# The last local head's four blocks tied behind the first four product steps, and the preceding head's blocks up to two a strip

## The chip, the cores and the metric

The kernel runs on one core of one Trainium2 chip. The metric is device time in microseconds of one launch; the time before is the median of three runs, 2186.0 us (2185.98 to 2188.91). Five engines of the core matter here: TensorE (PE for its matmuls, PEld for its weight loads), VectorE (DVE), ScalarE (ACT), GpSimd (POOL) and SyncE (SP), which issues all of this kernel's DMAs. Each engine runs its own instructions in the order in which they stand in its queue, and waits at an instruction until what it needs is there.

## The reference

One encoder layer is applied to a prompt of 1024 tokens and a sample of 256 tokens, each with 16 learned meta tokens in front. Eight heads attend globally (two key and value heads, rotary positions), eight heads attend to a neighbourhood of 8 x 16 grid cells and to the meta tokens. Both halves are gated and go through one output projection.

```python
def encoder_layer(h, norm_w, w_in, ..., rpb, w_out, rope_tabs):
    u = rms_norm(h, norm_w) @ w_in.astype(h.dtype)
    qa, ka, va, za, qb, kb, vb, zb = jnp.split(u, split_points(), axis=-1)
    ...
    ya = global_gqa(qa, ka, va) * jax.nn.silu(za)
    ...
    yb = neighbourhood_attention(qb, kb, vb, rpb) * jax.nn.silu(zb)
    y = jnp.concatenate([ya, yb], axis=-1) @ w_out.astype(h.dtype)
    return h + y
```

Here `qb`, `kb`, `vb`, `zb` are the query, key, value and gate of the eight local heads, 128 wide each.

## The kernel before

All products of the projections are made in three matmuls of a high and a low part each (`split`, L59: ACT casts the high part at L61, DVE subtracts for the low part at L62).

**Strips.** The input projection runs in two chunks of tokens. In each, a strip is one 128-wide slice of `w_in`, for instance the q of one head. `strips` (L176) loads and splits its weights in four pieces and multiplies them with all tokens of the chunk; in the second chunk a strip has two blocks of tokens (512 and 272 wide), so two PSUM tiles `pp`. An evacuation follows: `qk_evac` (L215) for q and k squares the strip on ACT (L218), sums over the partitions on POOL (L220), goes on with DVE and ACT (L221, L68 to L73), scales on DVE (L237) and stores the result in DRAM (L240); `z_evac` (L256) makes the gate.

**Chunk 2.** `chunk2` (L686) first does the global heads, and after each of these one strip of the list `late`. That list holds, for each local head, its strips v, k, q, z in this order (`VB`, `KB`, `QB_`, `ZB`); 24 of its 32 strips are left when the loop at L860 begins. I call the last four of them V7, K7, Q7 and Z7, after local head 7; they are strips 20 to 23 of that loop.

**Local blocks.** `local_blocks` (L820) is a generator over the eight local heads (0 to 7), four blocks each. A block is `attend_strip` (L416): four score products (L438) and the products with the meta tokens (L272, L273) into the PSUM tiles `sp` (two buffers); evacuation on DVE (L276, L443) into the tiles `S` (five buffers, two a block); the maximum by DVE and POOL (L452, L455, L282, L284); exponentials (L460, L463, L290); the sum (L452, L455, L299, L301); value products into `po` (L467, L470; one buffer); and `put_y` (L304), which ends with DVE's L318 and the store of y (L319). `load(h)` issues a head's loads: k from what K's strip stored (L777 to L780), v (L736), the bias table (L478), q (L789, L790) and z (L797); q is split anew on ACT and DVE after its load. The tiles of k, q and the table have one buffer each, so the loads for one head wait for the blocks of the head before. v's two tiles hold two blocks' windows each.

The loop at L860 projects one strip and then runs blocks as long as `done * n < 28 * (i + 1)`: 28 blocks over 24 strips. The 28th is head 6's last and is followed by `load(7)` inside the same step of the generator.

**Output projection.** `outproj` (L988) does the projection in seven products by a scheme that saves one of eight (`order = (1, 2, 5, 6, 7, 3, 4)`), each in ten steps; `step n` is 24 matmuls (`products`, L943: L949 to L951) into one PSUM tile `pq`. Two steps share one y tile (`y_load`, L880, `y_operand`, L894), and y tiles take turns in four buffers. Product 1 (steps 0 to 9) needs the global heads only; product 2 (from step 10) needs y of the local heads, where tile 0 (steps 10 and 11) holds blocks 0 and 1 of each head and tile 1 (steps 12 and 13) blocks 2 and 3. A step's weights `wm` are loaded into the tiles of the strips' input `xb` (L926) as these come free, and split. After steps 3 to 9 the generator is asked for a block, which is where head 7's four blocks are traced: behind steps 3, 4, 5 and 6.

**Order.** The program is written once in this traced order; a scheduler then orders each queue by a model of the time at which each instruction would be ready, with the traced order as priority, so that an instruction can be placed ahead of others that were traced before it. `issue_after(x)` adds one rule to it: instructions traced inside stand behind `x` in the queue of `x`'s engine. From step 10 on `in_order` (L869) keeps each queue in traced order.

Of the kernel before, what the change touches and what calls it, by code (L numbers as in the profile page):

```python
# [35 lines left out]
NH = 8  # L36
# [11 lines left out]
NT = TH // P  # L48
# [6 lines left out]
class Kern:  # L55
# [630 lines left out]
    def chunk2(self):  # L686
        nc, io = self.nc, self.io
# [16 lines left out]
        def k_strip(s, g, wc, rope):  # L704
            k, km = k_first(g)

            def evac(ps):
                for p, (o, n) in zip(ps, BL):
                    rp = (ct[:, o:o + n], st[:, o:o + n]) if rope else None
                    self.qk_evac(p, o, n, wc, rp, [(0, n, k[:, 0, C1P + o:C1P + o + n], k[:, 1, C1P + o:C1P + o + n])])  # L710
                return k, km
            return s, BL, evac

        def v_rows_of(s, g):

            def evac(ps):
                for p, (o, n) in zip(ps, BL):
                    self.rows_out(self.v_rows(p, o, n), n, self.vn[g], C1P + o)
            return s, BL, evac
# [9 lines left out]
        def v_windows(h):  # L729

            v = []
            for i in range(2):
                t = self.v.tile([P, 8, P], F32, tag=f"v{i}", name="vw", align_bytes=ALIGN)
                for j in range(2):
                    o = 32 * WIN0[2 * i + j]
                    nc.sync.dma_start(t[:, 4 * j:4 * j + 4, :], self.vn[2 + h][:].rearrange("(t p) d -> p t d", t=4)[o:o + P])  # L736
                    v.append(t[:, 4 * j:4 * j + 4, :])
            return v, self.load_vm(2 + h)
# [37 lines left out]
        def k_load(g):  # L776
            k = self.k.tile([P, NP + NMETA], F32, tag="k1", name="kfull", align_bytes=ALIGN)  # L777
            nc.sync.dma_start(k[:, :C1P], self.kfd[g][:, :C1P])
            nc.sync.dma_start(k[:, C1P:NP], self.k2d[g][:])
            nc.sync.dma_start(k[:, NP:], self.kfd[g][:, C1P:])  # L780
            km = self.k.tile([P, 8, NMETA], F32R, tag="km", name="km")[:, :7]
            full = [k[:, NP:].unsqueeze(1).to_broadcast([P, n, NMETA]) for n in (4, 3)]
            nc.scalar.copy(km[:, :4], full[0])
            nc.vector.tensor_tensor(out=km[:, 4:], in0=full[1], in1=km[:, :3].bitcast(F32), op=ALU.subtract)
            return k, km.rearrange("p c m -> p (c m)")

        def q_load(h):
            qf = self.qf.tile([P, NP], F32, tag="qf", name="qfull")
            nc.sync.dma_start(qf[:, :C1P], self.qfd[h][:])  # L789
            nc.sync.dma_start(qf[:, C1P:], self.q2d[h][:])  # L790
            q = self.q.tile([P, 2, NP], F32R, tag="q", name="q", align_bytes=ALIGN)
            self.split(q[:, 0, :], q[:, 1, :], qf[:])
            return q, qf

        def z_load(h):
            z = self.z.tile([P, NP], F32, tag="z", name="z")
            nc.sync.dma_start(z[:], self.zd[h][:])  # L797
            return z
# [4 lines left out]
        def run_block(h, b, q, z, k, v, tab):  # L803
            k, km = k
            v, vm = v
            if tab is not None:
                c = slice(64 * b, 64 * b + 64)
                q, qf = q
                self.attend_strip(q, qf, strips_of(z[:])[:, :, c], k, km, v[b], vm[:], tab, b,
                                  self.yd[1][:, b // 2:NP // P:2, h - 8, 64 * (b % 2):64 * (b % 2) + 64])  # L810
                return
            c = slice(QB * b, QB * b + QB)
            keys = [(k[:, 0, o:o + P], k[:, 1, o:o + P]) for o in range(0, NP, P)]
            self.attend(q[:, :, c], z[:, c], keys, km, v, vm[:], self.yd[0][:, 2 * b:2 * b + 2, h, :])
# [5 lines left out]
        def local_blocks():  # L820
            def load(h):
                k, v = k_load(2 + h), v_windows(h)
                tab, q, z = self.bias_table(h, "bt", (3, 384)), q_load(8 + h), z_load(8 + h)
                return q, z, k, v, tab

            tiles = load(0)
            for h in range(NH):
                for b in range(4):
                    run_block(8 + h, b, *tiles)
                    if b == 3 and h + 1 < NH:  # L830
                        tiles = load(h + 1)
                    yield

        pr = self.project
# [10 lines left out]
        for g in range(2):  # L845
            if g == 0:
                k, _ = pr(k_strip(KA, 0, kw, True), v_rows_of(VA, 0))
            else:
                k, = pr(k_strip(KA + g, g, kw, True))
                pr(v_rows_of(VA + g, g))  # L850
            v = v_tiles(g)
            for h in range(4 * g, 4 * g + 4):
# [3 lines left out]
                fill(FILL)  # L856

        self.blocks = local_blocks()
        n, done = len(late), 0
        for i in range(n):  # L860
            fill(1)
            while done < 4 * (NH - 1) and done * n < 4 * (NH - 1) * (i + 1):
                next(self.blocks)
                done += 1

# [75 lines left out]
    def products(self, ws, y):  # L943
        nc = self.nc
        ps = self.pq.tile([P, FB], F32, tag="pq", name="pq")
        for k in range(8):
            wh, wl = ws[k][:, 0, :], ws[k][:, 1, :]
            yh, yl = (a[k // WCH][:, k % WCH, :] for a in y)
            nc.tensor.matmul(ps[:], yh, wh, start=k == 0, stop=False)  # L949
            nc.tensor.matmul(ps[:], yh, wl, start=False, stop=False)  # L950
            nc.tensor.matmul(ps[:], yl, wh, start=False, stop=k == 7)  # L951
        return ps[:]

    def out_sums(self, p, i, ps, o):
# [33 lines left out]
    def outproj(self, end_attention):  # L988
        self.U, self.V = {}, {}
        order = (1, 2, 5, 6, 7, 3, 4)  # L990
        N = 2 * NT * len(order)

        def step(n):
            q, r = divmod(n, 2 * NT)
            return order[q], *divmod(r, 2)

        def tile_of(m):
            return order[m // NT], m % NT

        M = NT * len(order)  # L1000
        yr, ys, wr, ws, x, out = {}, {}, {}, {}, {}, {}

        def load_y(m):
            if m < M and m not in yr:
                yr[m] = self.y_load(*tile_of(m))

        def make_y(m):
            if m < M:
                load_y(m)
                ys[m] = self.y_operand(*tile_of(m), yr.pop(m))  # L1010

        def load_w(q, j):
            if q < len(order):
                wr[q, j] = self.w_load(order[q], j)

        def make_w(q, j):
            if q < len(order):
                ws[q, j] = self.w_operand(wr.pop((q, j)))

        load_y(0)  # L1020
        for j in range(16):
            if j == 12:
                load_y(1)
            load_w(0, j)
        make_y(0)
        for j in range(16):
            make_w(0, j)
        traced = None
        for n in range(N):
            p, t, b = step(n)  # L1030
            q, m = n // (2 * NT), n // 2
            if n == 2 * NT - 1:
                for _ in self.blocks:
                    pass
            if n == 2 * NT:
                end_attention()
                traced = len(self.nc.cur_bb.bb.instructions)
            if n - 2 in out:
                self.store(out.pop(n - 2), *step(n - 2))
            last = t == NT - 1  # L1040
            if NT - 3 <= t < NT - 1:
                with self.tc.issue_after(self.lasty):
                    for j in range(4):
                        load_w(q + 1, 8 * (t - NT + 3) + 4 * b + j)
            if q:
                for i in (n, n + 1, n + 2):
                    if i < N and i not in x:
                        x[i] = self.x_load(*step(i))
            direct = m + 1 < 2 * NT
            if direct:  # L1050
                (load_y, make_y)[b](m + 1)
            elif m + 2 < M:
                load_y(m + 2)
            if b == 0 and not direct:
                make_y(m + 1)
            ps = self.products([ws[q, 8 * b + k] for k in range(8)], ys[m])
            if last:
                for k in range(8):
                    make_w(q + 1, 8 * b + k)
            o = self.out_sums(p, 2 * t + b, ps, x.pop(n, None))  # L1060
            if o:
                out[n] = o
            if 2 < n < 2 * NT:
                next(self.blocks, None)
            if traced:
                traced = self.in_order(traced)
        for n in sorted(out):
            self.store(out[n], *step(n))
# [158 lines left out]
```

## Time and profile before

| what | value |
|---|---|
| median of three runs | 2186.0 us (2185.98 to 2188.91) |
| the profiled execution, whole | 2188.16 us |
| its span | 2186.4 us |
| granted TensorE clock, mean | 0.997 |
| TensorE busy | 2156.9 us, 99% of the span |
| DVE, ACT, POOL busy | 75%, 51%, 24% |
| matmuls of the strips 512 wide (L210 to L212) | 1664 a line, mean 0.39 us each |
| matmuls of the output projection (L949 to L951) | 560 a line, mean 0.39 us each |
| chain that ended last | TensorE 90%, DVE 3%, DMA 3% |

A timeline row holds the start and the length in us, the engine, the line, the operation, what it writes and reads, and how many instructions were merged; square brackets hold the engine's idle time just before and what released it. Matmuls overlap: one lasts 0.39 us though the next starts after 0.23. A window row holds, for a stretch of the span, its length and then the busy time (and the number of instructions) of PE, PEld, DVE, ACT and POOL, the granted clock as a share of full speed, the busy share of the DMA engines and GB/s. SPq rows are the issues of DMAs, which land some microseconds later. A group row holds line, engine, operation, tiles and count, then busy time in us and the mean of one in ns, then idle time before them.

### The profile page before, as it was taken

How to read it: one execution, taken by the hardware profiler on the slowest of the kernel's cores; microseconds unless marked ns; L12 is line 12 of the kernel's file. 1: busy time of each engine (PE TensorE's matmuls, PEld its weight loads, DVE VectorE, ACT ScalarE, POOL GpSimd, SP SyncE). 2: the span in 40 equal slices, each digit the busy share in tenths (PEclk: the TensorE clock that was granted, in tenths of full speed). 3: DMA queues.
4: the chain of work that ended last, by engine and by line, in shares of the span. 5: the costliest groups of instructions: out<-in, count | busy, mean ns of one | idle time of the engine just before them, and what ended most of it. 6: DMA issues, size and time to landing. Idle time of an engine off the chain costs nothing.

```text
span 2186.4 us, 34153 instructions
## 1 busy us (share of the span) xinstructions
PE 2156.9 (99%) x11736; PEld 1880.3 (86%) x11736; DVE 1644.7 (75%) x2991; ACT 1120.0 (51%) x2294; POOL 521.8 (24%) x249
## 2 busy tenths in 40 slices
PE   8999999999999999999999999999999989999999
PEld 7888888888888999998999999898889978788887
DVE  8687976787864889996799989777677686455763
ACT  6556544545554766665666666444444454232230
POOL 1232422222211233231233225333223221000000
PEclk9999999999999999999999999999999999999999
DMA  8767889988554333334233334654433463763663
GB/s 295 225 196 229 278 281 325 349 266 268 171 191 140 105 104 113 117 107 143 95 113 108 110 121 156 187 158 128 130 124 113 125 207 96 243 235 112 225 228 106
DMA packets 263614, 383.83 MB, mean 176 GB/s; under 512 B 45040, under 2 KB 113296, under 8 KB 263440
## 3 DMA queue, kind: packets, MB, share of 16 engines
q1 hardware_dynamic: 263440, 381.65, 53.9%
q8 instruction: 92, 1.51, 0.3%
q14 instruction: 82, 0.67, 0.1%
HBM read 281.01 MB, written 100.38 MB: 174 GB/s over the span
## 4 chain that ended last, share of the span: by engine, by line
PE 90%; DVE 3%; DMA 3%; ACT 1%; SPq 1%; issue 1%; POOL 1%; POOLq 0%; DVEq 0%; ACTq 0%
PE pp L210 20%; PE pp L212 20%; PE pp L211 20%; PE pq L949 6%; PE pq L951 6%; PE pq L950 6%; PE sp L438 2%; PE po L470 2%; PE sp L334 1%; PE sp L333 1%; PE sp L332 1%; PE po L372 1%; PE po L373 1%; PE po L374 1%; SPq L227 0%
## 5 line engine op out<-in xcount | busy, mean ns | idle before, releaser
L210 PE MATMUL pp<-x,wh 128*128 128x512 f32 (+1 forms) x1664 | 653.6, 394 | 6.3 <-ACT wh L61 6.2
L212 PE MATMUL pp<-x,wl 128*128 128x512 f32 (+1 forms) x1664 | 649.4, 391 | 0.2 <-DVE wl L62 0.2
L211 PE MATMUL pp<-x,wh 128*128 128x512 f32 (+1 forms) x1664 | 649.5, 391 | 0.0
L210 PEld LDWEIGHTS pp<-x,wh 128*128 128x128 f32 x1664 | 313.1, 188 | 63.0 <-ACT wh L61 7.5
L212 PEld LDWEIGHTS pp<-x,wl 128*128 128x128 f32 x1664 | 313.1, 188 | 62.1 <-DVE wl L62 1.2
L211 PEld LDWEIGHTS pp<-x,wh 128*128 128x128 f32 x1664 | 313.5, 188 | 52.1
L220 POOL PARTITION_ALL_REDUCE m<-ms x78 | 232.6, 2982 | 363.6 <-ACT ms L218 326.3
L62 DVE TENSOR_TENSOR wl<-wr,wh 128x512 fp32r<-128x512 f32 (+1 forms) x290 | 213.7, 740 | 131.0 <-ACT wh L61 104.2
L301 POOL PARTITION_ALL_REDUCE tot<-a x80 | 172.8, 2161 | 487.2 <-DVE a L299 466.9
L61 ACT CAST wh<-wr 128x512 fp32r<-128x512 f32 (+1 forms) x290 | 174.5, 607 | 199.2 <-PE pp L211 179.0
L211 PE MATMUL pp<-xb,wh 128*128 128x272 f32 x832 | 241.4, 290 | 0.0
L210 PE MATMUL pp<-xb,wh 128*128 128x272 f32 x832 | 240.0, 288 | 0.0
L212 PE MATMUL pp<-xb,wl 128*128 128x272 f32 x832 | 239.5, 288 | 0.0
L949 PE MATMUL pq<-wm,yh 128*128 128x512 f32 x560 | 219.7, 392 | 3.7 <-ACT yh L61 3.7
L951 PE MATMUL pq<-wm,yl 128*128 128x512 f32 x560 | 219.0, 391 | 0.0
L950 PE MATMUL pq<-wm,yh 128*128 128x512 f32 x560 | 218.8, 391 | 0.0
L284 POOL PARTITION_ALL_REDUCE ma<-m x80 | 107.6, 1345 | 440.8 <-DVE m L282 432.0
L210 PEld LDWEIGHTS pp<-xb,wh 128*128 128x128 f32 x832 | 156.6, 188 | 7.3
L211 PEld LDWEIGHTS pp<-xb,wh 128*128 128x128 f32 x832 | 156.5, 188 | 7.1
L212 PEld LDWEIGHTS pp<-xb,wl 128*128 128x128 f32 x832 | 157.4, 189 | 0.1
L949 PEld LDWEIGHTS pq<-wm,yh 128*128 128x128 f32 x560 | 105.8, 189 | 26.3 <-ACT yh L61 4.5
L951 PEld LDWEIGHTS pq<-wm,yl 128*128 128x128 f32 x560 | 105.5, 188 | 22.4 <-DVE yl L62 0.7
(207 smaller groups left out, 3845.0 us busy)
## 6 DMA issues: line engine op xcount, KB each, us to landing
wr<-in_w_in SPq DMA_DIRECT2D x414, 256.0 KB, 3.5
wld<-wl SPq DMA_DIRECT2D x132, 256.0 KB, 4.3
wl<-wld SPq DMA_DIRECT2D x132, 256.0 KB, 3.1
yr<-yd SPq DMA_DIRECT2D x35, 512.0 KB, 5.1
wq<-in_w_out SPq DMA_DIRECT2D x64, 256.0 KB, 5.2
td<-wq SPq DMA_DIRECT2D x64, 256.0 KB, 4.5
ww<-td SPq DMA_DIRECT2D x64, 256.0 KB, 5.3
ww<-in_w_out SPq DMA_DIRECT2D x48, 256.0 KB, 5.2
```

The lines of the kernel that those rows point to most:

```text
L61: self.hi = nc.scalar.copy(hi, full).ins
L62: return nc.vector.tensor_tensor(out=lo, in0=full, in1=hi.bitcast(F32), op=ALU.subtract).ins
L210: nc.tensor.matmul(p[:, :n], wh[:, k, :], xh[:, :n], start=first, stop=False)
L211: nc.tensor.matmul(p[:, :n], wh[:, k, :], xl[:, :n], start=False, stop=False)
L212: nc.tensor.matmul(p[:, :n], wl[:, k, :], xh[:, :n], start=False, stop=last)
L220: nc.gpsimd.partition_all_reduce(m2[:], ms[:], P, RED.add)
L284: nc.gpsimd.partition_all_reduce(ma[:], m1[:], P, RED.max)
L301: nc.gpsimd.partition_all_reduce(tot[:], a1[:], P, RED.add)
L438: nc.tensor.matmul(dst, k[:, o:o + P], qfv[:, a:e, :], start=True, stop=True)
L949: nc.tensor.matmul(ps[:], yh, wh, start=k == 0, stop=False)
L950: nc.tensor.matmul(ps[:], yh, wl, start=False, stop=False)
L951: nc.tensor.matmul(ps[:], yl, wh, start=False, stop=k == 7)
```

## The change

```diff
@@ local_blocks
                 for b in range(4):
                     run_block(8 + h, b, *tiles)
-                    if b == 3 and h + 1 < NH:
+                    if b == 3 and h + 2 < NH:
                         tiles = load(h + 1)
+                    yield
+                if h + 2 == NH:
+                    tiles = load(h + 1)
                     yield
@@ chunk2
             fill(1)
-            while done < 4 * (NH - 1) and done * n < 4 * (NH - 1) * (i + 1):
+            while done < 4 * (NH - 1) and done * n < 4 * (NH - 1) * (i + 1 + max(0, i + 5 - n) / 3):
                 next(self.blocks)
                 done += 1
+        next(self.blocks)
@@ products
-            nc.tensor.matmul(ps[:], yl, wh, start=False, stop=k == 7)
+            self.lastmm = nc.tensor.matmul(ps[:], yl, wh, start=False, stop=k == 7).ins
@@ outproj
-            if 2 < n < 2 * NT:
-                next(self.blocks, None)
+            if n < 2 * NT:
+                with self.tc.issue_after(self.lastmm):
+                    next(self.blocks, None)
```

Three things change. `load(7)` becomes a step of its own of the generator, taken after the last strip. The bound of the loop rises over the last four strips: with 24 strips, 25 blocks are done after strip 20 as before, then 27 instead of 26 after strip 21 (K7), 28 instead of 27 after strip 22 (Q7), and none is left for strip 23 (Z7). And head 7's four blocks are traced behind steps 0, 1, 2 and 3 of the output projection instead of 3, 4, 5 and 6, with their TensorE instructions kept behind the last matmul of that step in TensorE's queue; the other engines' instructions of a block are not tied. The instructions themselves, their number and their operands stay what they are.

## The prediction, made before the changed kernel ran

> **What bounds the kernel now.** I began with the page's first part.
>
> ```profile
> span 2186.4 us, 34153 instructions
> PE 2156.9 (99%) x11736; PEld 1880.3 (86%) x11736; DVE 1644.7 (75%) x2991; ACT 1120.0 (51%) x2294; POOL 521.8 (24%) x249
> ```
>
> TensorE is busy for all but 29.5 us of the span, and the change takes no matmul away. So it can win only idle time of TensorE and the half-clock time behind it. The view of waits, TensorE alone, says where the idle time is (total us, times, longest).
>
> ```profile
> PE sp L438 <- DVE m L452: 9.0, 1, 9.0
> PE pp L210 <- ACT wh L61: 6.2, 2, 5.4
> PE pq L949 <- ACT yh L61: 3.7, 1, 3.7
> PE tp L253 <- DVE vm L62: 1.7, 1, 1.7
> ```
>
> Two single waits, 9.0 and 3.7 us, lie on what the diff touches: a score matmul of a local block (L438) and a product step (L949). The view of windows gives the granted clock (behind the POOL column) after these two waits and after the one of 1.7 us.
>
> ```profile
> 1782.16:1786.12 3.96, 3.96 (x13) 3.65 (x14) 3.17 (x7) 2.39 (x5) 0.07 (x1) 0.50 0.29 98
> 1864.86:1868.01 3.15, 3.15 (x7) 2.43 (x8) 2.69 (x5) 0.62 (x1) 0.00 (x0) 0.50 0.81 283
> 612.65:618.00 5.35, 5.25 (x33) 4.66 (x34) 3.68 (x8) 1.95 (x4) 1.43 (x1) 1.00 0.53 165
> ```
>
> After the 9.0 us wait 3.96 us run at clock 0.50, which costs half of that, 1.98; after the 3.7 us wait 3.15 us, which costs 1.58; after 1.7 us of idleness nothing. With the waits' own 9.02 and 3.69 (rows below) the two places lose 16.3 us. That is the most the change can win at them.
>
> **The first wait.** The timeline of TensorE around it:
>
> ```profile
> 1752.09 0.61 PE L438 MATMUL sp<-qfull,kfull 128*128 128x128 f32 x4
> ...
> 1769.80 0.28 PE L467 MATMUL po<-Pm,vm 128*128 128x256 f32 x1
> ...
> 1771.64 0.61 PE L438 MATMUL sp<-qfull,kfull 128*128 128x128 f32 x4
> ...
> 1782.16 2.47 PE L438 MATMUL sp<-qfull,kfull 128*128 128x128 f32 x8 [9.02 <-DVE m L452]
> ...
> 1784.86 0.63 PE L949 MATMUL pq<-wm,yh 128*128 128x512 f32 x1
> ```
>
> I number the 32 local blocks in the order traced: 25 to 28 are head 6's, 29 to 32 head 7's. The rows at 1752.09 and 1771.64 are the scores of blocks 27 and 28, each behind a strip (Q7 and Z7, the last two); 1769.80 is block 27's value product. At 1782.16 stand block 29's scores, ahead of product step 0 (1784.86). TensorE runs its queue in order, so step 0 waits too. Was it ready? The vector engine's groups in the stretch of strip Z7, 1752.25 to 1771.64, say yes:
>
> ```profile
> L62 DVE TENSOR_TENSOR wm<-ww,wm 128x512 fp32r<-128x512 f32 x9 | 6.8, 771 | 0.0
> ...
> L62 DVE TENSOR_TENSOR yl<-yl,yh 128x512 fp32r<-128x512 f32 x2 | 1.3, 672 | 0.0
> ```
>
> Nine of the 16 weight splits and both halves of the first y tile start there; step 0 needs eight and those two. It sits out a wait that isn't its own.
>
> The releaser named, L452, doesn't feed L438. The timeline of the other engines and of the DMA queue shows whose wait it is:
>
> ```profile
> 1757.82 0.40 ACT L218 ACTIVATE ms<-pp 128x272 f32<-128x272 f32 x1
> ...
> 1776.65 0.49 DVE L237 SCALAR_TENSOR_TENSOR rs_r<-pp,nqkw,rs_r 128x272 f32<-128x272 f32 x1
> ...
> 1777.16 0.32 SPq L240 DMA_DIRECT2D q2d<-rs_r  x1
> ...
> 1778.90 0.32 SPq L790 DMA_DIRECT2D qfull<-q2d  x1
> ...
> 1782.10 1.04 ACT L61 CAST q<-qfull 128x1024 fp32r<-128x1024 f32 x1 [3.73 <-DMA qfull<-q2d]
> ```
>
> This is the second piece of head 7's q: squared out of PSUM at 1757.82, finished by DVE at 1777.14, stored, loaded again from 1778.90, landed when ACT's cast starts at 1782.10, 0.06 us ahead of the matmul. It is slow because DVE is full: the windows of strips Q7 and Z7 and of the gap (DVE is the third column of busy time).
>
> ```profile
> 1733.76:1752.25 18.49, 18.49 (x109) 16.51 (x108) 14.54 (x29) 8.30 (x19) 6.97 (x5) 1.00 0.28 87
> 1752.25:1771.64 19.39, 19.39 (x116) 17.38 (x115) 17.04 (x31) 12.93 (x26) 8.44 (x4) 1.00 0.68 235
> 1771.64:1782.16 10.52, 1.50 (x12) 1.23 (x11) 10.52 (x23) 6.71 (x16) 0.61 (x1) 0.70 0.69 241
> ```
>
> **The change, part by part.**
>
> *The tie.* Block 29's matmuls now follow step 0's last one in TensorE's queue. A step is 24 matmuls; a window of 100 us that holds nothing but product steps prices one at 100/440 = 0.227 us:
>
> ```profile
> 1900.00:2000.00 100.00, 100.00 (x440) 82.17 (x439) 53.13 (x76) 32.81 (x60) 0.00 (x0) 1.00 0.49 177
> ```
>
> So a step of 5.5 us moves into the gap. The wait does not vanish. Count from the scores behind strip Q7 (block 27's now, block 28's then, the same work): to the end of Z7 19.55 us (1752.09 to 1771.64), with step 0 25.0. The q tile lands 1782.10 - 1752.09 = 30.0 after the same point. I place block 29's scores right behind step 0, since the scheduler had them ready even ahead of it; they find 5.0 us still missing. Idle time falls from 9.02 to 5.0: gain 4.0. Step 0 has those 5 us of slack, so a late start of its own costs nothing up to there, and one for one beyond.
>
> Is the clock cold after 5.0 us? After 1.7 us it was not, after 3.69 it was; 5.0 lies beyond the second, so the 1.98 us stay. The Trainium skill, "TensorE: Matmul & The Clock Gate", Part 1: The HAM clock gate, has the array fall to half rate after an idle window of about 3.4 us; by it a rest just under that would stay warm, and the sum would then come out near 2173 us (an estimate from that page: 9.02 - 3.4 + 1.98 + 5.27 = 12.9 off 2186.0). The rows above agree with that window.
>
> *Two blocks behind strip K7, one behind Q7, none behind Z7.* Blocks 27 and 28 move up a strip; matmuls, vector and ACT work only change place. Block 28's scores go ahead of Z7 from behind it, which delays Q7's end and the q chain equally, so the count above holds. What it can cost is DVE time in strip Q7's stretch: a block's 17 vector instructions at some 0.42 us (L318's row, below) are 7.1 us, and that stretch has 18.49 - 14.54 = 3.95 free. At worst 3.2 us spill into the q chain, and the rest becomes 8.2; at best the chain has block 27's last rows out of its way and shortens by 2. I take zero: the loop's present rule already puts two blocks behind strips 0, 6, 12 and 18 (28(i + 1)/24, rounded up, rises by two there), and the list above has no entry for them. Around strip 18:
>
> ```profile
> L438 PE MATMUL sp<-qfull,kfull x32: 271/300/326, 1630.7 to 1677.1; 128*128 128x128 f32 x16, 128*128 128x192 f32 x16
> ```
>
> Four blocks of eight score matmuls in the 60 us from 1620, which hold some 3.2 strips.
>
> *load(7) as a step of its own behind the last strip.* It issues twelve DMAs: three for k, four for v, two for q, one each for vm, the bias table and z, all on SP's queue. What held k and q's first piece was block 28's scores; these would end some 18 us sooner, so k, that piece and the table (five issues, at L790's 0.32 us and up some 2 us) can pass ahead of the 16 w_out and four y loads. Bounds: nothing if SP is idle there, 2 us and the transfers' time if not, which step 0's slack covers. q's second piece still hangs on the store at 1777.16. I take zero.
>
> *Blocks 30 to 32 behind steps 1 to 3 instead of 4 to 6.* Today they already come one a step, at no wait:
>
> ```profile
> 1792.51 0.28 PE L467 MATMUL po<-Pm,vm 128*128 128x256 f32 x1
> ...
> 1815.17 0.61 PE L438 MATMUL sp<-qfull,kfull 128*128 128x128 f32 x4
> ...
> 1821.98 0.61 PE L438 MATMUL sp<-qfull,kfull 128*128 128x128 f32 x4
> ...
> 1829.24 0.60 PE L438 MATMUL sp<-qfull,kfull 128*128 128x128 f32 x4
> ...
> 1829.80 0.28 PE L467 MATMUL po<-Pm,vm 128*128 128x256 f32 x1
> ```
>
> 6.8 and 7.3 us apart: a step and a block each. I take zero.
>
> **The second wait** hangs on block 32's end:
>
> ```profile
> 1845.55 12.63 SPq L319 DMA_DIRECT2D yd<-y  x2
> ...
> 1857.37 0.42 DVE L318 SCALAR_TENSOR_TENSOR y<-y,r 128x256 f32<-128x256 f32 x1
> ...
> 1859.74 0.91 SPq L890 DMA_DIRECT2D yl<-yd  x2
> ...
> 1864.19 0.62 ACT L61 CAST yh<-yl 128x512 fp32r<-128x512 f32 x1 [8.05 <-DMA yl<-yd]
> ...
> 1864.86 0.79 PE L949 MATMUL pq<-wm,yh 128*128 128x512 f32 x1 [3.69 <-ACT yh L61]
> ```
>
> Block 32's y is done at 1857.79; its store and the one before hold SP's queue for 12.63 us; step 12's y tile is loaded only at 1859.74; its cast at 1864.19 releases L949. Three steps earlier is 16 us, less the 5 of rest; 4 would do. With no store ahead the load waits for its buffer alone, which step 9 frees two steps (11 us) before step 12. All of 3.69 + 1.58 = 5.27 goes. Next in line would be step 14's tile, which has the same 11 us.
>
> **Sum.** 4.0 + 5.27 = 9.3 us. The profiled execution took 2188.16 us, 1.76 of it around its span, and would take 2178.9. The median of the three runs, 2186.0, lies 2.2 lower; on that scale the forecast is **2176.7**.
>
> **Rivals.**
>
> A, *no wait left*: block 29's scores come behind step 1, or the q chain gains 5 us. For it: step 1's 5.5 us cover the 5.0. Against: the scheduler had those scores ready ahead of step 0, so they should follow it at once. Price: all 16.3 go, 2169.7.
>
> B, *the first gap stays*: the second block or the loads that pass push q or step 0's weights out by 4 us (the bounds above add to 5.2), and only the second wait goes: 2186.0 - 5.3 = 2180.7.
>
> C, *slower: the S buffers set the pace*. There are five, two a block, so block n+2 can't leave PSUM whole before block n's value product, and blocks advance one per half of the time from scores to value product. That time is 14.6 us for block 30 (1815.17 to 1829.80) but 20.9 for block 28 on a full DVE (1771.64 to 1792.51). At 20.9 the pace is 10.4 us against some 6.9 for a step with its block: 3.5 us of wait for each of blocks 30 to 32, and 1.6 of cold clock each time, 15.3 in all: 2186.0 - 9.3 + 15.3 = 2192.0. It decides from about 15 us on. For it: head 7 now starts while DVE still finishes Z7. Against: blocks 30 to 32 kept the pace without a wait. The Trainium skill, "TensorE: Matmul & The Clock Gate", Architectural detail, calls ACT's and DVE's queues strictly first in, first out, by which one waiting cast holds a block's whole chain; no row here contradicts it.
>
> D, *no change*: the scheduler pulls other work with a wait of its own into the gap, 2186.
>
> **Chances.** Forecast 0.52, A 0.20, B 0.14, C 0.08, D 0.06. A measurement of this kernel tells some 0.2%, 4.4 us, from no change: under 2181.6 is faster, over 2190.4 slower. The forecast, A and a third of B are faster: 0.77. C and a little of the tail of B and D are slower: 0.09. The rest, 0.14, is the same. The range runs from just under A, 2168.5, over the forecast's worst spill (3.2: 2179.9) and B to 2184; C, D and the tails of A and B lie outside. The forecast's own range is 2173 to 2180.
>
> **What would show it.** Right: step 0's first L949 directly behind strip Z7; then a rest of 3 to 7 us ahead of block 29's scores, still released by q's load, and clock 0.50 after it; no wait at step 12; TensorE idle for about 21.8 us of the span instead of 29.5. Wrong: block 29's scores behind step 1 (A), a wait for wm ahead of step 0 (B), waits at L438 or L467 between steps 1 and 6 (C).

## The result, and the profile after

| | before | after |
|---|---|---|
| median of six runs each | 2185.99 us | 2180.05 us |
| ratio, with its 95% interval | | 0.9966 [0.9956, 0.9975] |
| the profiled execution, its span | 2188.16, 2186.4 us | 2181.10, 2179.3 us |
| TensorE idle in the span | 29.5 us | 23.2 us |

The change is faster by 5.9 us of median, where 9.3 were forecast (2176.7); the profiled span is 7.1 us shorter. The lines of the products' matmuls are now L953 to L955, and a y tile's load is L894. The page's first part, of the kernel after:

```profile
span 2179.3 us, 34152 instructions
...
PE 2156.1 (99%) x11736; PEld 1881.0 (86%) x11736; DVE 1644.8 (75%) x2991; ACT 1120.7 (51%) x2294; POOL 520.8 (24%) x249
```

Of the 7.1 us, 6.3 are idle time of TensorE that is gone and 0.8 are busy time. Not all of it belongs to the change: strip Q7 starts behind the same 9742 matmuls in both kernels, at 1733.00 us after and at 1733.76 before, so 0.8 us had been gained before any moved block ran. The view of waits, TensorE alone, shows which (total us, times, longest):

```profile
PE po L467 <- DVE Pm L294: 6.8, 1, 6.8
PE pp L210 <- ACT wh L61: 5.4, 1, 5.4
...
PE sp L273 <- DVE q L62: 0.9, 1, 0.9
...
PE pq L953 <- ACT yh L61: 0.4, 1, 0.4
```

The second wait (3.69 us at step 12) is gone; the 0.4 us of the last row stand at a later step, at 1913.99 us. Of the first, 9.02 us at L438, 0.9 us are left at L273, but a new wait of 6.8 us stands at L467, a block's value product. TensorE's timeline around it:

```profile
1779.12 0.55 PE L467 MATMUL po<-Pm,vm 128*128 128x256 f32 x1 [6.79 <-DVE Pm L294]
...
1781.35 0.88 PE L953 MATMUL pq<-wm,yh 128*128 128x512 f32 x1
...
1787.42 0.60 PE L438 MATMUL sp<-qfull,kfull 128*128 128x128 f32 x4
...
1789.25 0.37 PE L273 MATMUL sp<-q,km 128*112 128x256 f32 x1 [0.89 <-DVE q L62]
```

Z7 ends at 1772.33. Behind it stands not step 0, as forecast, but the value product of block 28, head 6's last; step 0 (1781.35) follows it, and block 29's scores (1787.42) follow step 0. Why is block 28's Pm (its probabilities of the meta tokens) late? Rows of DVE, POOL and ACT from the timeline:

```profile
1765.45 0.40 DVE L282 TENSOR_TENSOR m<-m,Sm 16x256 f32<-16x256 f32 x1
...
1766.03 5.40 POOL L284 PARTITION_ALL_REDUCE ma<-m  x1 [3.40 <-DVE m L282]
...
1771.45 0.43 DVE L459 TENSOR_TENSOR S<-S,ma 128x256 f32<-128x256 f32 x1 [0.96 <-POOL ma L284]
...
1774.16 1.88 DVE L62 TENSOR_TENSOR wm<-ww,wm 128x512 fp32r<-128x512 f32 x3
...
1775.44 0.40 ACT L293 CAST Pm<-Sm 48x256 fp32r<-48x256 f32 x1
...
1778.56 0.41 DVE L294 TENSOR_TENSOR Pm<-Sm,Pm 16x256 fp32r<-16x256 f32 x1
...
1781.02 0.49 DVE L237 SCALAR_TENSOR_TENSOR rs_r<-pp,nqkw,rs_r 128x272 f32<-128x272 f32 x1
...
1786.88 1.05 ACT L61 CAST q<-qfull 128x1024 fp32r<-128x1024 f32 x1 [0.89 <-DMA qfull<-q2d]
```

Two things: the block's all-reduce takes 5.40 us, and then Pm's last instruction (L294, 1778.56), whose operand ACT has cast by 1775.84, waits its turn in DVE's queue behind weight splits (1774.16 is one group of them). Head 7's q is late in the same queue: its second piece leaves DVE at 1781.51 and lands at 1786.88. That is 34.3 us after the scores behind strip Q7 (1752.61), where it was 30.0 before. The windows of strips Q7 and Z7, of the wait and of what follows (DVE is the third busy time):

```profile
1733.00:1752.61 19.61, 19.61 (x117) 17.63 (x116) 17.52 (x37) 8.58 (x19) 7.85 (x6) 1.00 0.24 76
1752.61:1772.33 19.72, 19.72 (x117) 17.49 (x115) 17.54 (x33) 12.67 (x26) 11.73 (x4) 1.00 0.76 255
1772.33:1779.12 6.79, 0.00 (x1) 0.03 (x1) 6.73 (x15) 6.79 (x15) 0.00 (x0) 0.74 0.81 295
1779.12:1782.42 3.30, 3.30 (x12) 3.15 (x12) 3.30 (x7) 1.40 (x3) 0.00 (x0) 0.51 0.03 10
```

DVE works on through the wait, 6.73 of 6.79 us. Behind it 3.30 us run at clock 0.51, which costs 1.6. So the first place now costs 6.79 + 0.89 + 1.6 = 9.3 us, against 11.0 before: a gain of 1.7, where 4.0 had been forecast. The second place brought the forecast gain of 5.3. The two make 7.0, where the span behind 1733 us fell by 6.3; the later wait at 1913.99 is part of the difference.

### The profile page after: what moved, and what is told of

Its sections match the earlier page's. It is cut to its first block, busy times and chain, and to the rows that moved or that the text cites. A ratio compares the mean times of both kernels' runs of the same rounds, so it can differ in the third digit from the quotient of the medians.

```text
span 2179.3 us, 34152 instructions
## 1 busy us (share of the span) xinstructions
PE 2156.1 (99%) x11736; PEld 1881.0 (86%) x11736; DVE 1644.8 (75%) x2991; ACT 1120.7 (51%) x2294; POOL 520.8 (24%) x249
## 4 chain that ended last, share of the span: by engine, by line
PE 91%; DVE 3%; DMA 3%; ACT 1%; SPq 1%; issue 1%; POOL 1%; ACTq 0%; DVEq 0%; POOLq 0%
PE pp L210 21%; PE pp L211 21%; PE pp L212 21%; PE pq L953 5%; PE pq L955 5%; PE pq L954 5%; PE sp L438 2%; PE po L470 2%; PE sp L333 1%; PE sp L334 1%; PE sp L332 1%; PE po L372 1%; PE po L373 1%; PE po L374 1%; SPq L227 0%
## 5 line engine op out<-in xcount | busy, mean ns | idle before, releaser
L220 POOL PARTITION_ALL_REDUCE m<-ms x78 | 231.7, 2970 | 361.4 <-ACT ms L218 307.5
L953 PE MATMUL pq<-wm,yh 128*128 128x512 f32 x560 | 219.1, 391 | 0.4 <-ACT yh L61 0.4
L955 PE MATMUL pq<-wm,yl 128*128 128x512 f32 x560 | 218.3, 390 | 0.0
L284 POOL PARTITION_ALL_REDUCE ma<-m x80 | 110.3, 1378 | 414.1 <-DVE m L282 402.6
L953 PEld LDWEIGHTS pq<-wm,yh 128*128 128x128 f32 x560 | 105.3, 188 | 22.5 <-ACT yh L61 0.9
L955 PEld LDWEIGHTS pq<-wm,yl 128*128 128x128 f32 x560 | 105.3, 188 | 22.3 <-DVE yl L62 0.4
```

What stands on the lines that cost most here:

```text
L220: nc.gpsimd.partition_all_reduce(m2[:], ms[:], P, RED.add)
L284: nc.gpsimd.partition_all_reduce(ma[:], m1[:], P, RED.max)
L955: self.lastmm = nc.tensor.matmul(ps[:], yl, wh, start=False, stop=k == 7).ins
```

## The experiments

Each kernel was timed 5 to 11 times beside the kernel before on the same chip. There the kernel before ran 1 to 4 us slower (2187.11 to 2190.15 us), so only ratios are compared; 0.001 is 2.2 us. The theory at the start (theory D of the expectations): the steps' move ends the second wait, and what is left of the first is VectorE's lateness, which the loop's new bound makes worse.

### The parts of the change alone

`x1_loop_as_before` keeps the tie and the move to steps 0 to 3, and takes the loop's old bound:

```diff
-... (i + 1 + max(0, i + 5 - n) / 3):
+... (i + 1):
```

> The tie and the steps 0 to 3 as in the changed kernel, the loop over the last strips as before (blocks 26, 27, 28 behind strips K7, Q7, Z7). Theory D (VectorE: moving block 27's vector work into strip Q7's stretch made head 7's q and block 28's probabilities some 4 us late): q lands 30.0 us after the scores behind Q7, as before, instead of 34.3; Z7 19.55, block 28's scores 1.45 and step 0 5.5 make 26.5, so about 3.5 us of idleness stand before block 29's scores, with 1.5 for a cold clock at most, where before had 9.0 and 2.0; the second wait is gone. 2186.0 - 6.0 - 5.3 = 2174.7 us, 2173 to 2177. Rival (the tie alone brings the whole gain and the loop's change nothing): 2180, as the changed kernel.

Measured: 0.9978 [0.9969, 0.9987], where 0.995 was expected: a miss. Waits of TensorE:

```profile
PE po L467 <- DVE Pm L294: 4.9, 1, 4.9
PE sp L438 <- DVE m L452: 2.9, 1, 2.9
...
PE sp L273 <- DVE q L62: 0.7, 1, 0.7
...
PE sp L272 <- ACT q L61: 0.4, 1, 0.4
```

Step 0 does run in the gap. q lands 29.3 us after the scores behind strip Q7 (1782.9 against 1753.58), as the prediction had counted, and the waits for q come to 4.0 us, near its 5.0. But block 28's value product stands inside block 29's scores, and waits 4.9 us: in the kernel before, it came after the gap and had its Pm in time. The time is lost one instruction later.

`x2_loop_alone` has the change's loop and `load(7)`, but no tie, and the blocks behind steps 3 to 6 as before:

```diff
-            if n < 2 * NT:
-                with self.tc.issue_after(self.lastmm):
-                    next(self.blocks, None)
+            if 2 < n < 2 * NT:
+                next(self.blocks, None)
```

> The loop and load(7) as changed, but blocks 29 to 32 without the tie behind steps 3 to 6 as before. In TensorE's queue block 29's scores now stand behind step 3 on their own, and block 28's value product ahead of step 0. Theory D: the first wait is that of the value product, 6.8 us and 1.5 of cold clock, as in the changed kernel, and the second comes back, since block 32's value product stands half a step later than before: 3.7 to 6.4 us and 1.6. Near 2185 us, 2183 to 2188. Rival (the second wait went because the blocks moved up a strip, not because of the steps): 2180.

Measured: 1.0001 [0.9993, 1.001]. Waits of TensorE:

```profile
PE po L467 <- DVE Pm L294: 6.8, 1, 6.8
PE pq L953 <- ACT yh L61: 6.7, 2, 5.8
```

The loop alone brings nothing. It replaces the 9.0 us wait by the 6.8 at block 28's value product, and the second wait grows to 5.8 us.

`x7_steps_alone` is the kernel before with the blocks behind steps 0 to 3, untied (`if n < 2 * NT`).

> The kernel before with one edit: head 7's blocks are traced behind steps 0 to 3 instead of 3 to 6, no tie, the loop as before. Block 29's scores still stand ahead of step 0 in TensorE's queue, so the first wait stays at 9.0 us with 2.0 of cold clock, and the second, 3.69 and 1.58, goes: 2186.0 - 5.3 = 2180.7 us, 2179.5 to 2182. Rival (four blocks so early crowd VectorE and the steps wait for it): 2183 or more.

Measured: 0.9976 [0.9965, 0.9988], 5.2 us of 2186 (2.6 to 7.7 by the interval). Waits of TensorE:

```profile
PE sp L438 <- DVE m L452: 9.3, 1, 9.3
...
PE pq L949 <- ACT yh L61: 0.7, 1, 0.7
```

The first wait stays whole, the second goes (the 0.7 us stand at a later step, at 1913.65), and the time falls by what the prediction put on the second wait, 5.3 us. Most of the change's gain is this edit. Loop and tie together add some 0.001 to it (0.9966 against 0.9976); the intervals overlap.

### What the first place hangs on

`x3_steps_1_to_4` ties the blocks one step later (`if 0 < n < 2 * NT`), to give q another 5.5 us.

> The changed kernel with the tied blocks behind steps 1 to 4 instead of 0 to 3. Theory D: the wait of block 28's value product, 6.8 us and 1.5 cold, is VectorE's and stays; only the 0.9 us of block 29's scores for q goes: about 2179.2 us, 2178 to 2180.5. Rival (the wait of the value product is a matter of block 29 crowding VectorE and shrinks when that comes later): under 2177.

Measured: 0.9963 [0.9951, 0.9976]. L467's wait stays at 6.8 us, q's is gone. So q hardly counts in the changed kernel; the 6.8 us do.

`x8_value_28_behind_step_0` moves block 28's value product and the end of that block behind step 0. It leaves out one thing: the products with the meta tokens' v use head 7's, since `load(7)` has replaced the single tile `vm` by that point, so its output is not the layer's and only its time is of use.

```diff
+        def values():
+            po = self.op.tile([P, QB], F32, tag="po", name="po")
...
+        if self.defer:
+            self.deferred = values
+        else:
+            values()
...
                 with self.tc.issue_after(self.lastmm):
+                    if n == 0:
+                        self.deferred()
```

> The changed kernel with block 28's value product and put_y traced behind step 0 and tied there, ahead of block 29. Theory D: the wait of 6.8 us only hides another: step 0 starts directly behind Z7, and block 29's scores then wait for q, which lands as late as in the changed kernel, so 7 to 8 us of idleness stay, in another place: 2179 to 2181 us. Rival V (the value product ahead of step 0 is the loss itself): the 6.8 and 1.5 go, 2172.

Measured: 0.9966 [0.9954, 0.9979], as the change. TensorE now rests at another place, 4.8 us instead of 6.8, and no time is won. From its timeline, VectorE's evacuation of Z7's first half and TensorE's step 0 (the products' line is L961 here):

```profile
1773.86 0.67 DVE L259 TENSOR_TENSOR z<-pp,rb 128x512 f32<-128x512 f32 x1
...
1774.67 0.77 PE L961 MATMUL pq<-wm,yh 128*128 128x512 f32 x1 [4.79 <-DVE z L259]
```

Step 0 starts 0.14 us after L259 ends (1774.53). L259 reads strip Z7 out of the PSUM bank in which step 0 sums. `x4_both`, with the loop of x1 and the steps of x3, hits the second half of it:

> The loop as before and the tied blocks behind steps 1 to 4 instead of 0 to 3. Theory D: q lands 30.0 us after the scores behind Q7; Z7, block 28's scores and two steps are 32.0, so TensorE no longer waits for q at all, and block 32 still ends two steps earlier than before, so the second wait is gone too: all 16.3 us, 2169.7 us, 2168 to 2172. Rival (q comes later when more product work runs ahead of it, since VectorE and ScalarE serve the steps too): a wait of 3 us and more stays, 2174 or above.

Measured: 0.9967 [0.9955, 0.998], a miss of 0.004: q is no longer awaited, yet the gain is the change's. From its timeline, VectorE and TensorE:

```profile
1784.35 0.43 DVE L259 TENSOR_TENSOR z<-pp,rb 128x272 f32<-128x272 f32 x1
...
1784.93 0.77 PE L953 MATMUL pq<-wm,yh 128*128 128x512 f32 x1 [7.05 <-DVE z L259]
```

Here step 1 waits, until 0.15 us after L259 of Z7's second half (1784.78). The semaphore waits of this kernel as built say the same, in the count that DVE's semaphore has reached (step 1 also waits for a count of ACT):

```
step 0: bank 4, waits for DVE 2592    L259, Z7's first half:  bank 4, DVE 2592
step 1: bank 7, waits for DVE 2617    L259, Z7's second half: bank 7, DVE 2617
```

So three things that TensorE needs stand in one queue of VectorE: block 28's Pm, head 7's q, and the two L259 that free the banks of steps 0 and 1. `x6_weights_behind_q` is the change with the second eight weight splits, which only step 1 needs, put behind q's last instruction (L237) in that queue:

```diff
+            self.lastevac = nc.vector.scalar_tensor_tensor(...).ins
...
-        for j in range(16):
+        for j in range(8):
             make_w(0, j)
+        with self.tc.issue_after(self.lastevac):
+            for j in range(8, 16):
+                make_w(0, j)
```

> The changed kernel with one rule more: in VectorE's queue the low parts of the second eight weight tiles of product 1 stand behind the last instruction (L237) of head 7's q. Theory D: six splits less stand ahead of q's second piece (3.6 us) and about four less ahead of block 28's Pm (2.4 us): the wait of the value product shrinks from 6.8 to some 4.4, q is no longer waited for: 2176.9 us, 2175 to 2178.5. Rival L (loads): no change, 2180. Rival W (step 1 then waits for its weights): 2181 or more.

Measured: 0.9959 [0.9946, 0.9972]; span 2175.3 us against 2179.3. From the view of waits:

```profile
PE po L467 <- DVE Pm L294: 4.4, 1, 4.4
```

The wait is 2.4 us shorter, and 0.6 us of waiting for q stay: that part of the 6.8 was VectorE's order of work. In this kernel, too, block 28's all-reduce takes 5.40 us (timeline, below), 4.3 more than the usual 1.06, and 4.4 us of wait are left.

```profile
1763.31 5.40 POOL L284 PARTITION_ALL_REDUCE ma<-m  x1 [3.39 <-DVE m L282]
```

### Blocks earlier still

`x5_blocks_before_q7` runs block 25 behind the strip ahead of V7, blocks 26 and 27 behind V7 and block 28 behind K7, so that none is left for Q7 and Z7:

```diff
-... (i + 1 + max(0, i + 5 - n) / 3):
+... (i + 1 + 2 * max(0, i + 6 - n) / 3):
```

> The changed kernel with the loop's bound raised further: two blocks behind strips 20 and one more behind K7 (27 and 28 done by then), none behind Q7 and Z7. The loads of head 7's k, its first q piece and the bias table now issue even earlier. Theory D: strip Z7's stretch holds no block's vector work, so q's second piece lands some 6 us sooner, about 24 us after the end of Q7; Z7 and step 0 are 22.5; 1.5 us of idleness, no cold clock, no wait of a value product: 2171 us, 2169 to 2175. Rival L (the loads that pass ahead delay the weights of the output projection and with them VectorE): no better than the changed kernel, 2180.

Measured: 0.995 [0.9937, 0.9964], about half of the further gain that was expected. The window 1752 to 1785 us of the changed kernel:

```profile
1752.00:1785.00 33.00, 26.21 (x145) 23.41 (x144) 30.75 (x58) 21.49 (x44) 12.93 (x5) 0.90 0.70 236
```

The same window of x5:

```profile
1752.00:1785.00 33.00, 29.84 (x159) 25.91 (x158) 26.49 (x46) 20.73 (x40) 7.48 (x3) 0.95 0.73 244
```

DVE has 4.3 us less to do, and TensorE is busy 3.6 us more. The wait for Pm is gone; 3.2 us ahead of step 0 are left, here with a row of VectorE from the same timeline:

```profile
1777.71 0.68 DVE L259 TENSOR_TENSOR z<-pp,rb 128x512 f32<-128x512 f32 x1
...
1778.54 0.77 PE L953 MATMUL pq<-wm,yh 128*128 128x512 f32 x1 [3.16 <-ACT wm L61]
```

The profile names a cast of wm; but in the kernel as built step 0 waits for L259 and for casts that had ended by 1775.04, and L259 ends at 1778.39, again 0.15 us ahead. Two kernels were to move steps 0 and 1 into other banks, by two tiles taken from the pool and never used:

```diff
         traced = None
+        for _ in range(2):
+            self.pq.tile([P, FB], F32, tag="pq", name="pq")
```

> The kernel of x4_both, with two unused tiles taken from the pool of the product steps' PSUM banks ahead of the loop, so that steps 0 and 1 stand in the banks of strip Q7 and steps 2 and 3 in those of strip Z7. Nothing else is changed. Theory (a bank that VectorE frees late): in x4_both step 1 waited 7.1 us because its bank held the second half of Z7, which VectorE read at L259 only at 1784.4 us. With another bank step 1 starts directly behind step 0, at about 1777.5 us. But block 28's value product stands seven matmuls into step 1, and its Pm (L294) landed at 1789.8 us in x4_both; it hangs on the same VectorE queue, so the wait moves there, to 8.5 to 10.5 us at L467, and the ratio to before stays at 0.996 to 0.998 (x4_both: 0.9967). Rival (step 1 waited for its operands, the splits of wm and yl): the wait of about 7 us ahead of step 1 stays at L953.

> The kernel of x5_blocks_before_q7 (block 27 behind strip Z6's successor, block 28 behind K7, none behind Q7), with the two unused bank tiles of x9 and with the last head's blocks behind steps 1 to 4 instead of 0 to 3. Theory: the wait of 3.2 us ahead of step 0 in x5 ends 0.15 us after VectorE's L259 of Z7's first half (1777.71 + 0.68 us), whose bank step 0 takes, though the profile names a wm cast; in the bank of Q7 step 0 starts directly behind Z7 at about 1775.2 us, step 1 ends at about 1786.3 us, and q (1786.7 us in x5) is awaited for 0 to 0.7 us. x5's waits of 3.2 + 0.5 + 1.3 us and most of its cold clock go: the ratio goes from 0.995 to about 0.9925 (0.9915 to 0.994). Rival (the wm cast itself is awaited): the wait of about 3.2 us ahead of step 0 stays, and only the waits at block 29's scores go: 0.9943. Rival (VectorE is late with something else next, block 29's first Pm or step 3's bank): a new wait of 3 us or more, and 0.9945 to 0.996.

> x10_early_blocks_banks_moved without the two unused bank tiles, so that steps 0 and 1 stand in the banks of strip Z7 again. It measures the banks alone. Theory: step 0 waits about 3.2 us as in x5 (until L259 of Z7's first half, 1778.4 us), and step 1 about 1 us more for L259 of the second half (1785.2 us in x5); 0.9943 against 0.9925 for x10, 4 us. Rival (the banks cost nothing): the same ratio as x10 within 0.0008.

Measured: x9 0.9976 [0.9966, 0.9986], x10 0.9956 [0.9944, 0.9969], x11 0.9952 [0.9939, 0.9964]. x10 misses its forecast and x9's wait of 7.1 us stays at step 1, for the edit did nothing: the two unused tiles took no bank, and x9 and x10 have the instructions and banks of x4 and x11. So they tell nothing of banks, but they show how far one program's ratio scatters: 0.9967 and 0.9976, 0.9952 and 0.9956. x11 itself, for which 0.9943 was expected, is x5 with steps 1 to 4: step 0 waits 2.75 us, and starts 0.15 us after L259.

`x12_banks_read_before_splits` leaves the banks and puts L259 earlier: x11 with the edit of x6, but behind L259 of Z7's second half instead of L237.

> The kernel of x11_early_blocks_steps_1_to_4, with VectorE's halves of the second eight weight splits (wm 8 to 15, needed by step 1) put behind L259 of Z7's second half in VectorE's queue, where in x11 the two L259 stood among and behind the splits. Step 0's bank is the one of Z7's first half and step 1's that of its second half, and an unused tile takes no bank, which is why x9 and x10 ran as x4 and x11 did. Theory (steps 0 and 1 wait for VectorE to read Z7 out of their banks): the wait of 2.75 us ahead of step 0 goes (under 0.5 us is left), with most of the cold clock behind it; step 1 waits at most 1 us in all for its splits, which now come just ahead of it, and q is awaited for 0.3 to 1 us ahead of block 29: ratio 0.9935 (0.992 to 0.995) against 0.9952 for x11. Rival (the wm cast that the profile names is what step 0 awaits, the bank is not): the wait of about 2.7 us ahead of step 0 stays, and the ratio with it, 0.995 to 0.9957. Rival (VectorE has only so much time in this stretch): the wait at step 0 goes, but step 1 or block 29 waits 2.5 us or more for its splits or for q, and the ratio stays at 0.995 within 0.001.

Measured: 0.9962 [0.9948, 0.9975], where 0.9935 was expected: a miss. Its timeline, VectorE and TensorE:

```profile
1774.09 0.68 DVE L259 TENSOR_TENSOR z<-pp,rb 128x512 f32<-128x512 f32 x1
...
1774.91 0.47 PE L953 MATMUL pq<-wm,yh 128*128 128x512 f32 x1 [1.48 <-DVE z L259]
...
1778.72 0.69 DVE L62 TENSOR_TENSOR yl<-yl,yh 128x512 fp32r<-128x512 f32 x1 [3.96 <-ACT yh L61]
...
1781.43 0.43 DVE L259 TENSOR_TENSOR z<-pp,rb 128x272 f32<-128x272 f32 x1
1781.78 4.90 DVE L62 TENSOR_TENSOR wm<-ww,wm 128x512 fp32r<-128x512 f32 x8
...
1782.01 0.47 PE L953 MATMUL pq<-wm,yh 128*128 128x512 f32 x1 [1.41 <-DVE z L259]
...
1798.33 1.19 PE L438 MATMUL sp<-qfull,kfull 128*128 128x128 f32 x4 [3.36 <-DVE S L443]
```

With L259 earlier in the queue step 0's wait falls from 2.75 to 1.48 us, and both steps start 0.14 and 0.15 us after their L259: it is the bank, not the cast. But now VectorE idles 3.96 us at a split whose cast is not done, everything behind it shifts, and block 30's scores wait 3.36 us. The third theory of the expectation held: the wait went elsewhere, and the time did not fall.

The lowest ratio of all is x5's (0.995), with x11's and x10's beside it; all three beat the kernel before, and by their medians the change (0.9966) too, though the intervals overlap with the change's.

## Why the prediction came out as it did

**Right.** The two places, and that TensorE sat out a wait that wasn't step 0's own. The second wait went, all 5.27 us by the count, 5.2 in x7. Block 29's scores do follow step 0 at once, and the clock is cold behind the first rest, 3.30 us at 0.51. Neither C's waits nor A's came.

**Near by luck.** The measured 2180.05 is the forecast's worst spill (2179.9) almost to the digit, and rival B's price (2180.7). B's condition did hold, for q came 4.3 us later. But in both of them TensorE rests ahead of block 29's scores until q is there. It rested ahead of block 28's value product instead, which neither had looked at, and only 0.9 us were spent on q.

**Mis-sized: the first wait, 4.0 us of gain where 1.7 came.** The step that failed is "Two blocks behind strip K7, one behind Q7, none behind Z7": "At worst 3.2 us spill into the q chain", "I take zero". The spill was 4.3 us (34.3 after the scores behind Q7, not 30.0), 3.9 of them on DVE: its L237 ended 28.90 us after those scores, where it had ended after 25.05. With the old bound (x1) q lands after 29.3. And the count looked only at q, because q was what TensorE awaited in the kernel before. The bound took the free time of DVE in Q7's stretch alone. DVE stays nearly full through Z7's stretch and the wait, in which it also owes block 28's Pm. Before, that value product stood behind the gap, 1792.51, and had no wait to show.

**Missed: what is next in the queue.** x1 shows that it isn't the loop alone: with the old bound the waits for q are 4.0 us, where the forecast had 5.0, but 4.9 us of waiting for Pm come on top. x3, x4 and x8 each take one of the three needs away, and none gains over the change. The forecast's sign of being right, "step 0's first L949 directly behind strip Z7", did not come, for the same reason. The remedy that did gain is to give VectorE less to do there: x5 moves a block's work out of that stretch, and x6, by its median, orders it better.

**Open.** How much of L467's 6.8 us is the slow all-reduce: x6 separates the splits (2.4 us) from the rest (4.4), and the rest fits the 4.3 us by which that all-reduce was longer, but no kernel ran with that alone changed. The traces tie it to the loop: block 28's all-reduce takes 5.40 us in the kernels with the change's bound (the change, x2, x3, x6, x8) and 1.06 in those with the old one (before, x1, x4, x7). A short one is no cure by itself: in x1 Pm is late all the same.

## What to carry to other kernels

When a wait hides a full engine, list everything that the waiting engine needs from that queue over the next few steps, PSUM banks among it, and price the second and third arrivals before costing the removal of the first. A gap can be filled with a ready instruction only if nothing that is late stands ahead of it; moving work out of the full engine's stretch (x5) paid where reordering the waiting engine (x1, x4, x8) did not. Compare what the profile names as the releaser with the last instruction that ended just before the start.

## What the runs showed of the hardware

**The all-reduce and VectorE slow each other.** L284 takes 1.06 us in the median of the 26 blocks from 1412 us on, and up to 5.40 (one line of the program, in the changed kernel: count, then least, median and longest in ns, first and last start):

```profile
L284 POOL PARTITION_ALL_REDUCE ma<-m x26: 1062/1063/5396, 1412.8 to 1821.7; - x26
```

The 5.40 us are those of block 28, between 1766.03 and 1771.43, while VectorE runs instructions on tiles in SBUF, most of them subtractions of two, without a pause until L318 ends at 1770.50. The all-reduce ends 0.93 us after that. The other way round, VectorE's L462, 0.55 us in the median, takes 2.60 beside POOL's L220 (timeline of the changed kernel):

```profile
1752.00 3.29 POOL L220 PARTITION_ALL_REDUCE m<-ms  x1 [0.26 <-ACT ms L218]
...
1752.12 2.60 DVE L462 TENSOR_TENSOR S<-S,ma 128x384 f32<-128x384 f32 x1
```

The Trainium skill, "SBUF — State Buffer", section SBUF: two separate sides, says that GpSimd and a VectorE instruction with two operands in SBUF lock one pair of ports against each other for a whole instruction. The first row agrees with that. The second agrees in part: L462 ends at 1754.72, 0.57 us before L220 does. No run here took the ports apart from other causes.

**The start after a freed bank.** Six product steps that waited for L259 (x4, x5, x8, x11 and two in x12) started 0.14 to 0.15 us after it ended.

**A short rest can already halve the clock.** In the prediction's rows TensorE rests 1.7 us at no cost and 3.69 us at half clock afterwards. The runs show the edge lower, and not sharp. Rests of 2.75 us (x11, ahead of step 0), 2.90 (x1) and 3.16 (x5) are followed by half clock, though they are shorter than the 3.4 us of the prediction's estimate, so a rest just under that would hardly have stayed warm. Rests of up to 2.02 us (x5) mostly leave the clock at 1.00, but not always: at the same point of the program, L253, x3 rests 1.75 us and x4 1.78, and x3 alone runs at about half clock then. Windows behind the rests of x11, x3 and x4:

```profile
1776.89:1780.20 3.31, 3.31 (x8) 2.63 (x9) 2.96 (x6) 3.31 (x7) 0.00 (x0) 0.50 0.69 260
610.01:613.01 3.00, 3.00 (x13) 2.81 (x14) 2.85 (x7) 1.08 (x3) 1.42 (x1) 0.56 0.57 173
611.71:614.71 3.00, 3.00 (x20) 2.68 (x21) 2.85 (x7) 1.38 (x3) 1.42 (x1) 1.00 0.58 174
```

No run shows what decides it.
